# One of the four sums of K made by an accumulating DMA, in an attention kernel on one core

## The chip, the core and the metric

The kernel runs on one core of a Trainium2 chip. The core has five engines that run side by side, each with a queue of its own that it works through in order: TensorE (PE; its weight loads are listed as PEld), VectorE (DVE), ScalarE (ACT), GpSimd (POOL) and SyncE (SP). Transfers run on 16 DMA engines that all queues share. The metric is the time of one execution on the device in microseconds (us); of the kernel before there are three runs, of which the median counts.

## The reference

Attention without a mask, for eight batches of 2048 rows and a width of 512, in float32 from end to end:

```python
scores = np.matmul(q, k.transpose(0, 2, 1)) / np.sqrt(d_k)
attn_weights = special.softmax(scores, axis=-1).astype(np.float32)
return np.matmul(attn_weights, v)
```

## The kernel before

The kernel works in float16 with float32 sums in PSUM, and computes both products by a Strassen-Winograd scheme: a 2 x 2 block product is made of seven products instead of eight, from sums of the blocks. For the scores, the blocks of K are `a11, a12, a21, a22` (first index: which of two neighbouring blocks of 128 keys; second: the lower or upper half of the 512 columns) and those of Q are `b11` to `b22`. From K four sums are needed: `a21 + a22`, `a11 - a21`, `(a21 + a22) - a11`, and `a12` less the third.

K is held in four chunks of 512 keys. A chunk is loaded in float32 by POOL's queue and cast to float16 on the way (`load`, L133) into one of two staging buffers (`stage`), then transposed by a DMA of SP's queue into `kraw`, one buffer a chunk (`dma_transpose`, L159). The staging buffer comes free for a later load when that transpose has landed; Q goes the same way through the same two buffers. V is loaded by POOL's queue too (L220), without staging. In the first batch some of the transposes are done by PE.

The four sums of a chunk are made by DVE in `k_sums` (L190 to L199), one `tensor_tensor` each. L194 writes `a21 + a22` to a buffer of its own, `s1`. L195 then overwrites `a21` in place by `a11 - a21`. L196 makes `s2 = s1 - a11` and L197 `s4 = a12 - s2`. The seven products of a pair of key blocks are in `Group.product`: number 5 takes `s1` as weights, 6 `s2`, 3 `s4`, and 7 the overwritten `a21`; 1, 2 and 4 take the untouched blocks. A group's results are emptied from PSUM by ACT and DVE (L353 to L367; L364 after product 7, L367 after product 3) before the exponentials (L278).

The program is written out in one order, and each engine gets its instructions in that order; nothing reorders them later. The main loop runs over 32 quarters (`g`), four a batch, of 28 slots (and six more in which only what is left over is placed). In each slot stand, one after the other: one or two products of the scores of what comes next, the sums that a table names for the slot, products of the softmax weights with V, and then what `PLAN` names: loads and transposes for the next batch. The order of the score products over seven slots is `QORDER`: product 1 of a new group, 7 of the one before, 5 and 6 of the new one, 4 of the old one, 3 and 2 of the new one.

The tables are `SUMS` (one text for each quarter of a batch) and `SUMS_AT` (the same for the quarters 0, 1 and the last two). A word such as `k03@14` means: sum 3 in the list that `k_sums(0)` returns, at slot 14. So `k?1` to `k?4` are the four lines of that list, L194 to L197 in the kernel before. Chunks 0 and 1 of the next batch are first used in the third quarter, from slots 0 and 14 on, chunks 2 and 3 in the fourth, likewise. Words with N, L and S are sums of the softmax weights (L395 to L398), x, y, z those of an inner scheme (L588 to L591), q and v those of Q and V.

`PLAN` places, as (quarter, slot) in a batch: the loads of K at (0,18), (0,24), (1,8) and (1,16), their transposes at (1,0), (1,8), (1,20) and (2,7); the loads of Q for the next half at (2,0) and (2,15), their transposes at (2,14) and (2,26); loads of V at (0,14), (1,12), (2,6) and (2,20). POOL has besides these the additions of two output halves (L555). Where two loads stand back to back in POOL's queue, the second is issued as soon as its own waits and POOL allow.

Of the kernel before, what the change touches and what calls it, by code (L numbers as in the profile page):

```python
# [12 lines left out]
def kernel(  # L13
# [21 lines left out]
    nc = tc.nc  # L35
# [7 lines left out]
    ADD = mybir.AluOpType.add  # L43
# [9 lines left out]
    CH = 4  # L53
# [29 lines left out]
    def bank(name):  # L83
        name = "pz" if name == "py" else name
        t = psum[name].tile([P, 512], F32, tag=name)
        return t
# [10 lines left out]
    kops = []  # L97
# [78 lines left out]
    def pe_transpose(what, c, n0=0, n1=CH):  # L176
        for n in range(n0, n1, 2):
            transposed(what, c, n, 2, nc.scalar.copy if n and n0 != n else nc.vector.tensor_copy)

    def k_blocks(c):  # L180
        w = kops[c][0][:].rearrange("p (j s) c r -> p j s c r", s=2)
        return w[:, :, 0, 0:2], w[:, :, 0, 2:4], w[:, :, 1, 0:2], w[:, :, 1, 2:4]

    def q_blocks(sp):
        w = qraw[sp % 2]
        return w[:, 0:NT, 0:2], w[:, NT:2 * NT, 0:2], w[:, 0:NT, 2:4], w[:, NT:2 * NT, 2:4]

    add, sub = nc.vector.tensor_add, nc.vector.tensor_sub

    def k_sums(c):  # L190
        a11, a12, a21, a22 = k_blocks(c)
        _, s1, s2, s4 = kops[c]
        return [
            lambda: add(s1[:], a21, a22),  # L194
            lambda: sub(a21, a11, a21),  # L195
            lambda: sub(s2[:], s1[:], a11),  # L196
            lambda: sub(s4[:], a12, s2[:]),  # L197
        ]

    def t3_of(sp):  # L200

        if sp:
            return q_blocks(sp)[1]
        t = pts[1][0][1][:].rearrange("p j q -> p (j q)")[:, 0:NT * 2 * P]
        return t.rearrange("p (n c r) -> p n c r", n=NT, c=2)

    def q_sums(sp):
        b11, b12, b21, b22 = q_blocks(sp)
        t1, t2, t4 = qsum
        return [  # L210
            lambda: sub(t1[:], b12, b11),
            lambda: sub(t2[:], b22, t1[:]),
            lambda: sub(t3_of(sp), b22, b12),
            lambda: sub(t4[:], b21, t2[:]),
        ]
# [56 lines left out]
    def new_p(sp):  # L272
        left = ppool.tile([P, 2, NJ, QH], F16, tag="left", name="left")
        right = ppool.tile([P, NJ, 2, QH], F16, tag="right", name="right")
        pts[sp] = ((left[:, 0], left[:, 1]), right, left)
# [4 lines left out]
    def plain_tile(kb, half, name):  # L280

        st = bank(name)
        c, n = divmod(kb, CH)
        for dc in range(ND):
            nc.tensor.matmul(  # L285
                st[:], kops[c][0][:, n, dc, :], qraw[0][:, half * NT:(half + 1) * NT, dc, :],
                start=(dc == 0), stop=(dc == ND - 1),
            )
        left, right = pts[0][0:2]
        exp(right[:, kb // 2, kb % 2, :] if half else left[kb % 2][:, kb // 2, :], st[:])  # L290
# [19 lines left out]
    class Group:  # L310
# [6 lines left out]
        def product(self, n):  # L317
            c, j = divmod(self.j, 2)
            a11, a12, a21, a22 = k_blocks(c)
            b11, b12, b21, b22 = q_blocks(self.sp)  # L320
            _, s1, s2, s4 = kops[c]
            t1, t2, t4 = qsum
            t3 = t3_of(self.sp)
            if n == 1:
                if self.sp not in pts:
                    new_p(self.sp)
                self.left, self.right = pts[self.sp][0:2]
                self.x = bank("qx")
            elif n == 5:
                self.z = bank(self.own + "z")  # L330
            lhs, rhs, dst = {
                1: (a11, b11, "x"),
                2: (a12, b21, "y"),
                3: (s4, b22, "z"),
                4: (a22, t4, "x"),
                5: (s1, t1, "z"),
                6: (s2, t2, "x"),
                7: (a21, t3, "x"),
            }[n]
            dst = getattr(self, dst)  # L340
            for dc in range(2):
                nc.tensor.matmul(  # L342
                    dst[:], lhs[:, j, dc, :], rhs[:, :, dc, :],
                    start=(n in (1, 5) and dc == 0), stop=(dc == 1),
                    skip_group_check=True,
                )
            getattr(self, f"after{n}", lambda: None)()
# [259 lines left out]
    def fine(g, s, part):  # L607
# [38 lines left out]
        if part == 1:  # L646
            product(1, xb[:, 0:P])
            product(5, xb[:, P:P + W5])
            nc.scalar.copy(out=xa[:, 0:P + W], in_=xb[:, 0:P + W])
        elif part == 2:  # L650
            product(6, xb[:, 0:P])
            nc.scalar.copy(out=cs[:, 0], in_=xb[:, 0:P])  # L652
            product(2, xa[:, 0:P])
        elif part == 3:
            product(3, xa[:, P:P + W])
            product(7, xb[:, 0:P])
            nc.scalar.copy(out=cs[:, 1], in_=xb[:, 0:P])
            nc.vector.tensor_add(xa[:, P:H], xa[:, P:H], cs[:, 0])
            done(pa)
        else:  # L660
            product(4, xb[:, 0:P])
            nc.vector.tensor_add(xb[:, P:H], xb[:, P:H], cs[:, 1])
            done(pb)
# [17 lines left out]
    def placed(text):  # L681

        at = {}
        for word in text.split():
# [27 lines left out]
    SUMS = (  # L712
# [9 lines left out]
    )  # L722
    SUMS_AT = {
# [3 lines left out]
        ),  # L727
        1: (
            "z1@0 Z1@1 z2@1 Z2@1 Z3@2 S2@3 z4@5 Z4@5 x1@7 S3@9 z3@9 S4@9 x2@11 x3@13 x4@13 k01@15 "
            "k03@15 y1@16 y3@17 k04@18 y2@18 Y1@18 y4@18 k02@18 Y2@20 N1@21 Y4@21 Y3@22 N3@24 q1@27 "  # L730
            "q2@27"
        ),
        NP - 2: (
# [30 lines left out]
    background = deque()  # L764
# [13 lines left out]
    def sum_of(g, x):  # L778

        b, qt = divmod(g, NQT)  # L780
        sp = g // 2 + 1 + g % 2
        nb = b + (qt == NQT - 1)
        n = int(x[-1]) - 1
        if x[0] == "q":
            f = sp < NP // 2 and q_sums(sp)
        elif x[0] == "k":
            f = (b + 1 < B or g == 0) and k_sums(int(x[1]))
        elif x[0] == "v":
            f = nb < B and v_sums(nb, *map(int, x[1:-1]))
        elif x[0] in "XYZW":  # L790
            f = nb < B and vi_sums(nb, "XYZW".index(x[0]))
        elif x[0] in "xyzw":
            f = a_sums(g, "xyzw".index(x[0]))
        elif x[0] == "N":
            f = g + 1 < NP and p_sums(g + 1, "ab", 0, NE if g % 2 else NJ)
        elif x[0] == "L":
            f = p_sums(g, "ab", NE)
        elif x[0] == "S":
            f = p_sums(g, "ab")
        else:  # L800
            f = p_sums(g, x[0].lower(), NG if x[0] == "a" else 0)
        if f:
            f[n]()
# [79 lines left out]
    def step(n=1):  # L883
        for _ in range(min(n, len(background))):
            background.popleft()()


    for n, (kb, half) in enumerate([(kb, 0) for kb in range(4, 8)] + [(kb, 1) for kb in range(8)]):
        if (kb, half) == (5, 0):
            pe_transpose("k", 1, 2, 4)  # L890
        if (kb, half) == (6, 0):
            pe_transpose("q", 1)
            background.extend(q_sums(0))
        if (kb, half) == (3, 1):
            pe_transpose("k", 2)
        if (kb, half) == (6, 1):
            pe_transpose("k", 3)
            background.extend(k_sums(3))
        plain_tile(kb, half, "qz" if n % 3 == 2 else "qx")
        if (kb, half) in ((3, 1), (7, 1)):  # L900
            background.extend(k_sums(kb // CH))
        step(2)
    prev = None
    tiles = [(kb, half) for kb in range(8, 12) for half in range(2)]
# [84 lines left out]
```

## Time and profile before

| | before |
|---|---|
| time, median of 3 runs | 794.21 us (793.92 to 794.26) |
| span of the profiled execution, first to last instruction | 792.4 us |
| PE busy | 786.1 us |
| DVE busy | 712.4 us |
| ACT busy | 646.3 us |
| POOL busy | 124.1 us |
| packets of POOL's DMA queue (q0), share of 16 engines | 42.2% |
| packets of SP's DMA queue (q1), share of 16 engines | 39.0% |

The page and the views shown below come from one execution that the hardware profiler recorded. It gives a span, not a time of the kind that the three runs have; the median lies 1.8 us above it. An instruction's row has its start, its duration, engine, line and operation, what it writes and reads, and in brackets how long its engine stood idle before it, and what ended that. A row of a group has a count, the busy time and the mean, then the idle time. A row of the waits has the time waited in total, how often, and the longest. A row of a DMA queue has its packets, its megabytes and the time its packets took as a share of the 16 engines. A row of DMA issues ends with the time from issue to landing.

### The profile page before, as it was taken

The numbers are of one execution on the slowest core, as the hardware profiler recorded it, in microseconds if no ns is written. First come the engines' busy times: TensorE is split into PE (matmuls) and PEld (weight loads), VectorE is DVE, ScalarE is ACT, GpSimd is POOL, SyncE is SP. The second block draws the span as 40 slices with busy tenths as digits, with TensorE's granted clock in tenths as the row PEclk, the third lists the DMA queues.
The fourth block names the chain that finished last, engine by engine and source line by source line (L and its number), as shares of the span: only waits on it lengthen the run. The fifth ranks groups of instructions, "written<-read, shape, count | busy, mean of one in ns | idle before, by whom it ended". The sixth has DMA issues, their size and how long they took to land.

```text
span 792.4 us, 17987 instructions
## 1 busy us (share of the span) xinstructions
PE 786.1 (99%) x6574; PEld 536.6 (68%) x6574; DVE 712.4 (90%) x1562; ACT 646.3 (82%) x1339; POOL 124.1 (16%) x166
## 2 busy tenths in 40 slices
PE   9999999999999999999999999999999999999998
PEld 5556666666666666666666676666666666666686
DVE  3789999989999899998999989999899998999864
ACT  4678888888888888888988888888888888888862
POOL 4011111121121120211202121022210222100000
PEclk9999999999999999999999999999999999999999
DMA  9989991999929996399965999379991999911112
GB/s 222 180 149 187 159 192 35 175 199 166 180 43 186 209 176 134 71 195 180 172 130 106 193 189 180 82 136 200 163 202 55 151 195 178 195 35 47 49 66 95
DMA packets 206456, 116.05 MB, mean 146 GB/s; under 512 B 124320, under 2 KB 205344, under 8 KB 206368
## 3 DMA queue, kind: packets, MB, share of 16 engines
q0 software_dynamic: 49648, 49.29, 42.2%
q1 hardware_dynamic: 156432, 65.30, 39.0%
q8 instruction: 51, 0.84, 0.4%
q10 hardware_dynamic: 288, 0.33, 0.1%
q14 instruction: 37, 0.30, 0.1%
HBM read 100.73 MB, written 33.55 MB: 169 GB/s over the span
## 4 chain that ended last, share of the span: by engine, by line
PE 96%; DVE 2%; ACT 1%; issue 1%; DVEq 0%; ACTq 0%
PE t L342 45%; PE t L447 29%; PE t L634 17%; PE t L285 2%; DVE cz L367 1%; DVE ks L196 1%; PE tr L169 1%; PE tr L146 0%; PE t L853 0%; PE t L301 0%; DVE right L397 0%; ACT right L278 0%; ACT o L456 0%; ACT left L278 0%; DVE s L396 0%
## 5 line engine op out<-in xcount | busy, mean ns | idle before, releaser
L456 ACT ACTIVATE o<-t,r 128x256 f32<-128x256 f32 x314 | 143.9, 480 | 88.0 <-DVE r L482 33.2
L342 PE MATMUL t<-qraw,kraw 128*128 128x512 f16 x728 | 198.0, 379 | 0.1
L278 ACT ACTIVATE left<-t 128x512 f16<-128x512 f32 (+1 forms) x260 | 154.4, 601 | 12.0 <-PE t L342 5.8
L342 PE MATMUL t<-qs,ks 128*128 128x512 f16 x488 | 138.7, 379 | 0.1
L278 ACT ACTIVATE right<-cz 128x1024 f16<-128x1024 f32 x122 | 129.9, 1065 | 1.0 <-DVE cz L364 0.8
L342 PEld LDWEIGHTS <-kraw 128*128 128x128 f16 x976 | 87.1, 97 | 57.9 <-issue 0.6
L447 PEld LDWEIGHTS <-right 128*128 128x128 f16 x1024 | 99.5, 98 | 38.3 <-DVE right L397 2.7
L447 PEld LDWEIGHTS <-s 128*128 128x128 f16 x1072 | 102.1, 97 | 30.5 <-issue 0.3
L634 PEld LDWEIGHTS <-si 128*128 128x128 f16 x1044 | 75.4, 97 | 39.4 <-issue 1.4
L555 POOL TENSOR_TENSOR o<-o 128x256 f32<-128x256 f32 x58 | 51.1, 882 | 307.9 <-ACT o L456 221.2
L367 DVE TENSOR_TENSOR cz<-t,cz 128x512 f32<-128x512 f32 x122 | 83.8, 686 | 15.3 <-ACT o L456 6.7
L342 PEld LDWEIGHTS <-ks 128*128 128x128 f16 x732 | 67.9, 97 | 40.2 <-issue 0.2
L358 ACT COPY cz<-t 128x512 f32<-128x512 f32 x120 | 70.5, 587 | 26.2 <-PE t L342 25.2
L364 DVE TENSOR_TENSOR cz<-t,cz 128x512 f32<-128x512 f32 x122 | 83.5, 684 | 4.0 <-PE t L342 3.6
L634 PEld LDWEIGHTS <-left 128*128 128x128 f16 x928 | 66.2, 97 | 20.6
L459 DVE SCALAR_TENSOR_TENSOR o<-t,r,o 128x256 f32<-128x256 f32 x134 | 62.5, 478 | 19.0 <-ACT ci L652 6.4
L353 ACT COPY t<-t 128x512 f32<-128x512 f32 x120 | 69.9, 583 | 3.2 <-PE t L342 0.8
L447 PE MATMUL t<-vt,s 128*128 128x256 f16 (+1 forms) x560 | 72.5, 273 | 0.0
L342 PE MATMUL t<-qs,kraw 128*128 128x512 f16 x244 | 72.5, 378 | 0.0
L342 PE MATMUL t<-qraw,ks 128*128 128x512 f16 x244 | 72.4, 378 | 0.0
L361 ACT COPY cz<-t 128x512 f32<-128x512 f32 x122 | 71.2, 583 | 0.3
L634 PE MATMUL t<-vh,left 128*128 128x128 f16 x696 | 67.3, 219 | 0.0
(101 smaller groups left out, 1239.1 us busy)
## 6 DMA issues: line engine op xcount, KB each, us to landing
out_dram<-o SPq DMA_DIRECT2D x256, 128.0 KB, 2.5
vh<-in_v_dram POOLq DMA_DIRECT2D x32, 512.0 KB, 10.6
stage<-in_q_dram POOLq DMA_DIRECT2D x28, 512.0 KB, 7.1
stage<-in_k_dram POOLq DMA_DIRECT2D x28, 512.0 KB, 7.6
right<-in_q_dram POOLq DMA_DIRECT2D x2, 512.0 KB, 9.9
right<-in_k_dram POOLq DMA_DIRECT2D x2, 512.0 KB, 12.0
first<-in_q_dram SPq DMA_DIRECT2D x2, 256.0 KB, 3.7
cz<-in_q_dram SPq DMA_DIRECT2D x2, 256.0 KB, 4.7
```

The source lines that it names most:

```text
L278: nc.scalar.activation(out=out_, in_=in_, func=EXP, scale=inv_sqrt_d)
L342: nc.tensor.matmul(dst[:], lhs[:, j, dc, :], rhs[:, :, dc, :], start=(n in (1, 5) and dc == 0), stop=(dc == 1), skip_group_check=True,)
L353: f(out=self.y[:], in_=self.x[:])
L358: f(out=self.cz[:, 1, :], in_=self.z[:])
L361: nc.scalar.copy(out=self.cz[:, 0, :], in_=self.x[:])
L364: nc.vector.tensor_add(self.cz[:, 1, :], self.x[:], self.cz[:, 1, :])
L367: nc.vector.tensor_add(self.cz[:, 0, :], self.z[:], self.cz[:, 0, :])
L447: nc.tensor.matmul(dst[:, 0:width], lhs(j), rhs(j), start=(first and j == 0), stop=(j == NJ - 1), skip_group_check=True,)
L456: nc.scalar.activation(out=out_, in_=src, func=COPY, scale=r[:])
L459: nc.vector.scalar_tensor_tensor(out=out_, in0=src, scalar=r[:], in1=out_, op0=MULT, op1=ADD)
L555: nc.gpsimd.tensor_add(self.o11, self.o11, more)
L634: nc.tensor.matmul(dst, lhs[:, j, :], rhs[:, j, :], start=(n == 1 and j == 0), stop=(j == NI - 1), skip_group_check=True,)
```

## The change

`a21 + a22` is made in place, in `a21`, by a DMA of POOL's queue that reads `a22` and adds it to what is there. `a11 - a21`, which needs the old `a21`, is therefore made first and goes to the buffer that `s1` had, now called `s3`. `s2` is made from the new `a21`. For three chunks of the first batch (0, 1 and 3) the addition stays on DVE, in place; chunk 2 of that batch and all four of each later one are made by the DMA, 29 in all. Products 5 and 7 take their weights from the exchanged places. In the tables the words are placed anew: `k?2`, which was the last of a chunk's four, stands right behind `k?1`.

```diff
+    def by_dma(out_, in_):
+        nc.gpsimd.dma_start(out=out_, in_=in_, accum_op=ADD)
+
+    def k_sums(c, first=False):
         a11, a12, a21, a22 = k_blocks(c)
-        _, s1, s2, s4 = kops[c]
+        _, s3, s2, s4 = kops[c]
         return [
-            lambda: add(s1[:], a21, a22),
-            lambda: sub(a21, a11, a21),
-            lambda: sub(s2[:], s1[:], a11),
+            lambda: sub(s3[:], a11, a21),
+            lambda: add(a21, a21, a22) if first else by_dma(a21, a22),
+            lambda: sub(s2[:], a21, a11),
             lambda: sub(s4[:], a12, s2[:]),
         ]
...
-                5: (s1, t1, "z"),
+                5: (a21, t1, "z"),
                 6: (s2, t2, "x"),
-                7: (a21, t3, "x"),
+                7: (s3, t3, "x"),
...
-            background.extend(k_sums(3))
+            background.extend(k_sums(3, True))
...
-            background.extend(k_sums(kb // CH))
+            background.extend(k_sums(kb // CH, True))
```

The words of K in the tables, by quarter of a batch:

| place | before | after |
|---|---|---|
| first quarter of all (`g` 0) | k21@17 k22@18 k23@22 k24@27 | the same |
| second quarter of all (`g` 1) | k01@15 k03@15 k04@18 k02@18 | k01@15 k02@15 k03@20 k04@20 |
| second quarter | k01@11 k03@14 k04@18 k02@18 | k01@11 k02@11 k03@18 k04@18 |
| third quarter, chunk 1 | k11@14 k13@15 k14@17 k12@18 | k11@4 k12@4 k13@14 k14@15 |
| third quarter, chunk 2 | k21@17 k22@19 k23@26 k24@27 | k21@17 k22@17 k23@26 k24@27 |
| fourth quarter, chunk 3 | k31@1 k33@8 k34@10 k32@18 | k31@1 k32@1 k33@8 k34@10 |

More of the change, by code (lines that the diff above doesn't have):

```diff
@@ L188 @@
     add, sub = nc.vector.tensor_add, nc.vector.tensor_sub
-    def k_sums(c):
+    def by_dma(out_, in_):
+        nc.gpsimd.dma_start(out=out_, in_=in_, accum_op=ADD)
+    def k_sums(c, first=False):
         a11, a12, a21, a22 = k_blocks(c)
-        _, s1, s2, s4 = kops[c]
+        _, s3, s2, s4 = kops[c]
         return [
-            lambda: add(s1[:], a21, a22),
-            lambda: sub(a21, a11, a21),
-            lambda: sub(s2[:], s1[:], a11),
+            lambda: sub(s3[:], a11, a21),
+            lambda: add(a21, a21, a22) if first else by_dma(a21, a22),
+            lambda: sub(s2[:], a21, a11),
             lambda: sub(s4[:], a12, s2[:]),
@@ L320, in product @@
             b11, b12, b21, b22 = q_blocks(self.sp)
-            _, s1, s2, s4 = kops[c]
+            _, s3, s2, s4 = kops[c]
             t1, t2, t4 = qsum
@@ L729 @@
             "z1@0 Z1@1 z2@1 Z2@1 Z3@2 S2@3 z4@5 Z4@5 x1@7 S3@9 z3@9 S4@9 x2@11 x3@13 x4@13 k01@15 "
-            "k03@15 y1@16 y3@17 k04@18 y2@18 Y1@18 y4@18 k02@18 Y2@20 N1@21 Y4@21 Y3@22 N3@24 q1@27 "
+            "k02@15 y1@16 y3@17 y2@18 Y1@18 y4@18 k03@20 k04@20 Y2@20 N1@21 Y4@21 Y3@22 N3@24 q1@27 "
             "q2@27"
```

12 rows, old and new, of the table SUMS are left out of this document.

## The prediction, made before the changed kernel had run

> **What bounds the kernel now.** I read the page's busy times first, then who waits for whom, then narrow stretches of the timeline of each engine around the sums of K.
>
> ```profile
> span 792.4 us, 17987 instructions
> PE 786.1 (99%) x6574; PEld 536.6 (68%) x6574; DVE 712.4 (90%) x1562; ACT 646.3 (82%) x1339; POOL 124.1 (16%) x166
> ```
>
> PE is busy for all but 6.3 us, so work taken from another engine can win at most those. DVE, at 90%, runs just behind PE: a stall on it soon becomes a stall of PE. Two rows of the waits, one of PE's weight loads and one of POOL, show where there is no slack.
>
> ```profile
> PEld L447 <- DVE right L397: 2.7, 7, 0.4
> ```
>
> ```profile
> POOL stage L133 <- DMA kraw<-stage: 149.2, 18, 13.8
> ```
>
> Seven times, once a batch, PE waits 0.4 us for L397 on DVE: there DVE sets the pace. And POOL's in-order queue stands for up to 13.8 us at a load (L133) that needs a staging buffer back from a DMA transpose of K. The change puts DMAs into that queue, and DVE will wait for them.
>
> **The change, part by part.** *Removed:* 29 of the 32 additions `a21 + a22` on DVE (three of the first batch stay there).
>
> ```profile
> L194 DVE TENSOR_TENSOR ks<-kraw 128x512 f16<-128x512 f16 x32 | 15.7, 490 | 1.1 <-ACT kraw L172 0.8 <-DMA kraw<-stage 0.2
> ```
>
> 29 x 0.49 = 14 us of DVE's 712. I count this as nothing: PE is full beside them. If they were what PE waits for, the gain would be the 2.7 us above at most, and that wait hangs on a chain without them, shown below. *Moved, at nothing:* `a11 - a21`, same size, goes to the buffer that held the sum; PE's products 5 and 7 swap operands of equal shape.
>
> *Added:* 29 accumulating DMAs of 128 KB on POOL's queue, four a batch, each of which waits for `k?1` on DVE, and after each a wait of DVE: `k?3` reads the sum. So each is late or not by three things: what POOL does before it, what its ring still holds, and where `k?3` stands. The nearest rows for the first two are a pair of loads that POOL issues back to back (timeline of POOL; then the issues of the two, with the us to landing):
>
> ```profile
> 393.59 0.74 POOL L133 DMA_DIRECT2D stage<-in_q_dram  x1 [13.43 <-DMA kraw<-stage]
> 394.32 0.75 POOL L220 DMA_DIRECT2D vh<-in_v_dram  x1
> ```
>
> ```profile
> stage<-in_q_dram POOLq DMA_DIRECT2D x1, 512.0 KB, 7.5
> vh<-in_v_dram POOLq DMA_DIRECT2D x1, 512.0 KB, 10.3
> ```
>
> The first lands at 401.1, the second, issued 0.7 later, at 404.6: 3.5 us apart. They don't share the engines, they go one after the other. An accumulating DMA issued behind a load will land after it. How long it then takes, d, no row shows. The queues' packets in three stretches of 1 us (365 to 366, 400 to 401, 393 to 394):
>
> ```profile
> q0 software_dynamic: 163, 0.15, 89.1%
> q1 hardware_dynamic: 166, 0.04, 30.9%
> ```
>
> ```profile
> q0 software_dynamic: 198, 0.20, 122.4%
> ```
>
> ```profile
> q1 hardware_dynamic: 1133, 0.29, 127.5%
> ```
>
> POOL's queue (q0) moves 198 packets, 0.20 MB, in a us alone, 163 beside transposes. `a21` is two runs of 512 B in each of 128 partitions: 256 packets. Bounds: by bytes 0.128/0.20 = 0.65 us; if every run counts twice, being read from two places, 512/163 = 3.1 us. I take 256/198 = 1.3, since time here follows packets. And q1's transposes fall from 1133 packets to 166 beside q0, so each us that q0 works longer costs a transpose under way 0.85 us: c = 0.85 d = 1.1 (0.55 to 2.7).
>
> [...]
>
> *Place A, chunk 2, third quarter of a batch.* `k22@17` comes behind the load of q at (2,15), the one that stood 13.43 us above for the transpose of chunk 3. So POOL can issue it only at 394.33 although `k21` is done long before, and it lands d after 401.1. DVE's rows (start, us), then PE's:
>
> ```profile
> 398.75 0.72 DVE L196 TENSOR_TENSOR ks<-ks,kraw 128x512 f16<-128x512 f16 x1
> 399.50 0.43 DVE L197 TENSOR_TENSOR ks<-kraw,ks 128x512 f16<-128x512 f16 x1
> 399.84 0.42 DVE L397 TENSOR_TENSOR right<-left,right 128x512 f16<-128x512 f16 x1
> ```
>
> ```profile
> 399.38 1.32 PE L447 MATMUL t<-vh,right 128*128 128x256 f16 x8
> 400.54 0.59 PE L342 MATMUL t<-qs,ks 128*128 128x512 f16 x2
> ```
>
> `k23` (L196) keeps its place, 398.75, before the load has landed. Queued behind it are `k24` and L397, for which PE's L447 waits already, the 0.4 us above. No slack: what `k23` is late, PE is late. The seven batches differ; the first and the last of them (POOL's issue, its landing, `k23`):
>
> ```profile
> 103.06 0.74 POOL L133 DMA_DIRECT2D stage<-in_q_dram  x1 [10.53 <-DMA kraw<-stage]
> ```
>
> ```profile
> stage<-in_q_dram POOLq DMA_DIRECT2D x1, 512.0 KB, 6.8
> ```
>
> ```profile
> 110.20 0.71 DVE L196 TENSOR_TENSOR ks<-ks,kraw 128x512 f16<-128x512 f16 x1
> ```
>
> ```profile
> 680.29 0.74 POOL L133 DMA_DIRECT2D stage<-in_q_dram  x1 [12.86 <-DMA kraw<-stage]
> ```
>
> ```profile
> stage<-in_q_dram POOLq DMA_DIRECT2D x1, 512.0 KB, 5.6
> ```
>
> ```profile
> 687.07 0.71 DVE L196 TENSOR_TENSOR ks<-ks,kraw 128x512 f16<-128x512 f16 x1
> ```
>
> Landing less `k23`: 103.06 + 6.8 - 110.20 = -0.34 in the first, -1.18 in the last; worked out alike, all seven are -0.34, 1.80, -0.30, 2.34, -1.05, -1.49, -1.18. To each comes d, and c, because `k12@4` is now in front of the load of v that runs beside the transpose of chunk 3 for which POOL stands. With d + c = 2.4: 2.1 + 4.2 + 2.1 + 4.7 + 1.4 + 0.9 + 1.2 = 16.6 us.
>
> *Place B, chunk 0, second quarter.* `k02@11` comes behind the load of k at (1,8); `k03@18` takes the place that `k04` had (L197). First and last of the six like batches (issue, landing, L197), with what follows on DVE and PE in the first:
>
> ```profile
> 168.50 0.78 POOL L133 DMA_DIRECT2D stage<-in_k_dram  x1 [7.77 <-DMA kraw<-stage]
> ```
>
> ```profile
> stage<-in_k_dram POOLq DMA_DIRECT2D x1, 512.0 KB, 8.1
> ```
>
> ```profile
> 173.67 0.42 DVE L197 TENSOR_TENSOR ks<-kraw,ks 128x512 f16<-128x512 f16 x1
> ```
>
> ```profile
> 175.82 0.69 DVE L367 TENSOR_TENSOR cz<-t,cz 128x512 f32<-128x512 f32 x1 [0.42 <-ACT cz L361]
> ```
>
> ```profile
> 178.09 0.59 PE L342 MATMUL t<-qs,ks 128*128 128x512 f16 x2
> ```
>
> ```profile
> 649.37 0.78 POOL L133 DMA_DIRECT2D stage<-in_k_dram  x1 [7.87 <-DMA kraw<-stage]
> ```
>
> ```profile
> stage<-in_k_dram POOLq DMA_DIRECT2D x1, 512.0 KB, 7.9
> ```
>
> ```profile
> 654.45 0.42 DVE L197 TENSOR_TENSOR ks<-kraw,ks 128x512 f16<-128x512 f16 x1
> ```
>
> The load lands 168.50 + 8.1 - 173.67 = 2.93 us after that place, 2.82 in the last; all six: 2.93, 2.68, 0.06, 2.71, 1.31, 2.82. Here is some cover. Behind `k03` stand two short sums, `k04` and a reciprocal, then L367, which empties the bank that PE's product 5 (178.09) overwrites: L367 would start 1.2 and end 1.9 us after the landing, so PE bears a landing up to 176.2, 2.5 past the place. Per batch lateness + 1.3 - 2.5: 1.7 + 1.5 + 0 + 1.5 + 0.1 + 1.6 = 6.4 us. Without the cover it would be 20.
>
> *Chunks 1 and 3, at nothing.* `k12@4` is issued behind the load of q at (2,0), `k32@1` when `k31` and an addition of POOL are done:
>
> ```profile
> 378.64 0.78 POOL L133 DMA_DIRECT2D stage<-in_q_dram  x1 [0.65 <-issue]
> ```
>
> ```profile
> stage<-in_q_dram POOLq DMA_DIRECT2D x1, 512.0 KB, 7.9
> ```
>
> ```profile
> 387.52 0.41 DVE L194 TENSOR_TENSOR ks<-kraw 128x512 f16<-128x512 f16 x1
> ```
>
> ```profile
> 406.57 0.41 DVE L196 TENSOR_TENSOR ks<-ks,kraw 128x512 f16<-128x512 f16 x1
> ```
>
> The first lands at 386.5 + 1.3, 0.3 after `k13`'s new place (387.52, where `k11` was); its product comes two slots later. The second has v's landing, 404.6 + 2 x 1.3 = 407.2, against `k33` at 406.57 plus what PE has lost at A just before. With d = 3.1 both would add some 4 us. The first batch's own order I leave out.
>
> *The sum:* 16.6 + 6.4 = 23 on the profiled span, 815.4. The median shown, 794.2, lies 1.8 above the span; so 817.2. The bounds of d give 8.5 + 3.7 = 12 us (806) and 40 + 16 = 56 us (851); with d and c at zero 4.1 + 1.1 us would still be lost (799.5).
>
> **The rivals.** *Faster:* the accumulating DMA doesn't stand behind the load's packets.
>
> ```profile
> out_dram<-o SPq DMA_DIRECT2D x256, 128.0 KB, 2.5
> ```
>
> A store of the same 128 KB lands in 2.5 us; issued at 394.33 the sum would be there at 396.8, 1.9 before `k23`, and at B too. It decides at 4.4 us from issue to landing. DVE then has 14 us less to do, and the kernel ends at 794.2 - 2.7 = 791.5 if all the waits for L397 go. Against it stands the order in which the two loads landed, and that L397's chain at A holds none of the removed additions. [...]
>
> *No change:* in time as above, and nothing won, 794.2. For it speaks how full PE is within a batch (stretch, us, then busy time of PE, PEld, DVE, ACT and POOL):
>
> ```profile
> 351.80:447.90 96.10, 95.99 (x819) 65.55 (x817) 90.24 (x201) 82.02 (x173) 16.20 (x21) 1.00 0.89 153
> ```
>
> *Much slower:* each run is read twice and the DMA takes 3.1 us, 851. For it, only that the packets of q0 go at 163 in a us beside transposes; against it, that 256 are enough for the bytes.
>
> **How the numbers follow.** The forecast, late at A and B with d near 1.3 (799 to 832), 0.62; much slower (832 to 856) 0.18; faster 0.14; no change 0.06. 0.2%, 1.6 us, is about what a measurement of this kernel can tell from no change; so faster 0.14, same 0.06, slower 0.80. The range 798 to 842 leaves out the faster cases and the top of the slow ones; the likeliest case's own is 806 to 832.
>
> **What would show it.** In the profile after, DVE should wait for a DMA into kraw at the line of `k?3`, longest in the third quarter, and PE should stand as long for L397; fewer but similar waits in the second, none over a us for chunks 1 and 3. The accumulating DMAs of chunks 0 and 2 should land 7 to 10 us after issue, those of chunk 3 earlier. If they land in 2 to 4 us, the queueing is wrong and with it the sign; if DVE waits and PE doesn't, the cover is larger than I read it; if waits at A are over 5 us, d is.

## The result, and the profile after

| | before | after |
|---|---|---|
| time, median | 794.07 us (793.69 to 794.26, 4 runs) | 834.25 us (830.25 to 839.31, 4 runs) |
| span of the profiled execution | 792.4 us | 837.5 us |
| ratio, with its 95% interval | | 1.0508 (1.0463 to 1.0554) |

The changed kernel is slower by 40 us. The prediction had said 817.2, with 798 to 842 as its range. In the experiments below a time is the median of all runs of a kernel and a ratio is that of its fast runs, which leaves out one run of four, over 1.5% above the fastest, in two of the kernels (with 841.55 and 810.61 us). In the rows of the changed kernel every line from L190 on has moved down: `k?1` to `k?4` are L197 to L200, the DMA is L191, L342 of before is L345, L364 is L367, L367 is L370, L397 is L400 and L447 is L450. The head of its page, and its rows of POOL's and SP's DMA queues and of the new DMA:

```profile
span 837.5 us, 18029 instructions
...
PE 799.0 (95%) x6574; PEld 539.5 (64%) x6574; DVE 702.3 (84%) x1533; ACT 642.9 (77%) x1339; POOL 161.5 (19%) x195
```

```profile
q0 software_dynamic: 57536, 53.09, 45.0%
q1 hardware_dynamic: 156432, 65.30, 38.1%
```

```profile
kraw<-kraw POOLq DMA_DIRECT2D x29, 128.0 KB, 6.6
```

The change does what it says: 29 instructions fewer on DVE, 29 DMAs more, and DVE's busy time falls from 712.4 to 702.3 us. PE does the same 6574 matmuls, but stands: what isn't PE's busy time grew from 6.3 us (792.4 - 786.1) to 38.5 (837.5 - 799.0), that is by 32.2. The other 12.9 us of the 45.1 by which the spans differ are PE's busy time itself, 786.1 to 799.0. Who waits for whom, in the waits of the changed kernel:

```profile
DVE ks L199 <- DMA kraw<-kraw: 55.5, 19, 6.2
...
PEld L345 <- DMA kraw<-kraw: 16.1, 6, 3.9
...
PE t L345 <- DMA kraw<-kraw: 14.4, 6, 3.6
...
PE t L345 <- DVE cz L370: 10.8, 5, 3.5
...
PEld L450 <- DVE right L400: 3.6, 7, 1.2
```

DVE stands 55.5 us at `k?3` for the new DMA, as forecast. But PE's waits aren't where the forecast had most of them. L450 for L400, the chain of place A (chunk 2, third quarter), is 3.6 us, against 2.7 before. PE waits at L345 instead, in part for the DMA itself. DVE's timeline in one batch, at places B (chunk 0), C (as I call chunk 1 from here, `k13@14` of the third quarter) and A:

```profile
388.71 0.42 DVE L199 TENSOR_TENSOR ks<-kraw 128x512 f16<-128x512 f16 x1 [5.87 <-DMA kraw<-kraw]
...
414.57 0.43 DVE L199 TENSOR_TENSOR ks<-kraw 128x512 f16<-128x512 f16 x1 [4.89 <-DMA kraw<-kraw]
...
426.12 0.71 DVE L199 TENSOR_TENSOR ks<-kraw 128x512 f16<-128x512 f16 x1
```

Added up over the batches, DVE waits 28.2 us at B, 22.3 at C, 1.1 at A, 1.5 at chunk 3 and 2.4 once in the first batch. PE's timeline in the same batch:

```profile
390.52 0.81 PE L345 MATMUL t<-qs,kraw 128*128 128x512 f16 x2 [3.18 <-DVE cz L370]
...
414.60 1.02 PE L345 MATMUL t<-qs,kraw 128*128 128x512 f16 x2 [3.61 <-DMA kraw<-kraw]
```

The first gap is the chain foreseen for B: the DVE row L370 behind `k03` empties the bank that product 5 needs. The second chain is shorter: product 5 of chunk 1 reads the sum itself. And both matmuls took longer (0.81 and 1.02 us; 0.59 in the undisturbed rows). Stretches of 1 us of the changed kernel (busy time of PE, PEld, DVE, ACT and POOL, then PE's granted clock, DMA share and GB/s):

```profile
389.00:390.00 1.00, 0.00 (x0) 0.00 (x0) 1.00 (x5) 0.09 (x1) 0.00 (x0) 1.00 1.17 89
390.00:391.00 1.00, 0.48 (x2) 0.20 (x2) 1.00 (x3) 1.00 (x3) 0.00 (x0) 0.88 0.87 103
391.00:392.00 1.00, 0.76 (x6) 0.43 (x5) 1.00 (x3) 1.00 (x4) 0.00 (x0) 0.50 0.17 45
392.00:393.00 1.00, 1.00 (x9) 0.83 (x7) 1.00 (x2) 0.68 (x2) 0.58 (x1) 0.50 0.45 148
393.00:394.00 1.00, 1.00 (x7) 0.74 (x5) 0.00 (x0) 0.97 (x1) 0.17 (x1) 0.50 1.71 130
394.00:395.00 1.00, 1.00 (x7) 0.47 (x6) 0.62 (x2) 0.33 (x2) 0.00 (x0) 0.91 0.42 88
```

After the gap of 3.18 us PE runs at half its clock for 3.4 us. The trace has four such stretches, at 308, 390, 414 and 496; one less the granted clock, summed over slices of 1 us, is 1.7 us for each of the first three and 3.4 for the last, 8.5 in all. The kernel before has none.

Last, the landings. These are POOL's timeline and then three answers on its issues (the last number is us from issue to landing): the load of q at (2,0), chunk 1's DMA behind it, and the transpose of chunk 3 that SP issued at the same time.

```profile
400.45 0.79 POOL L133 DMA_DIRECT2D stage<-in_q_dram  x1 [1.00 <-DVE o L462]
403.03 1.19 POOL L191 DMA_DIRECT2D kraw<-kraw  x1 [1.79 <-PE t L345]
```

```profile
stage<-in_q_dram POOLq DMA_DIRECT2D x1, 512.0 KB, 6.9
```

```profile
kraw<-kraw POOLq DMA_DIRECT2D x1, 128.0 KB, 11.5
kraw<-stage SPq DMA_TRANSPOSE x1, 15.1
```

The load lands at 407.3 and the DMA, issued 2.6 us after the load's issue, at 414.5: 7.2 us behind the load, not 1.3. The transpose, issued at 402.94, is under way until 418.0.

### The profile page after: what moved, and what is told of

It is laid out like the page before. It is cut to its first block, busy times and chain, and to the rows that moved or that the text cites. A ratio compares the mean times of both kernels' runs of the same rounds, so it can differ in the third digit from the quotient of the medians.

```text
span 837.5 us, 18029 instructions
## 1 busy us (share of the span) xinstructions
PE 799.0 (95%) x6574; PEld 539.5 (64%) x6574; DVE 702.3 (84%) x1533; ACT 642.9 (77%) x1339; POOL 161.5 (19%) x195
## 3 DMA queue, kind: packets, MB, share of 16 engines
q0 software_dynamic: 57536, 53.09, 45.0%
## 4 chain that ended last, share of the span: by engine, by line
PE 73%; DMA 17%; DVE 4%; ACT 3%; issue 2%; POOL 0%; DVEq 0%; POOLq 0%; ACTq 0%
PE t L345 34%; PE t L450 23%; DMA kraw<-kraw 14%; PE t L637 12%; DMA kraw<-stage 4%; PE t L288 2%; DVE ks L199 1%; ACT right L281 1%; ACT left L281 1%; ACT o L459 1%; DVE cz L370 1%; PE tr L169 1%; PE tr L146 0%; PE t L856 0%; PE t L304 0%
## 5 line engine op out<-in xcount | busy, mean ns | idle before, releaser
L345 PE MATMUL t<-qs,kraw 128*128 128x512 f16 x488 | 147.6, 384 | 25.4 <-DMA kraw<-kraw 14.4
L345 PE MATMUL t<-qraw,ks 128*128 128x512 f16 x484 | 144.3, 380 | 1.7 <-ACT cz L361 1.2
L345 PE MATMUL t<-qraw,kraw 128*128 128x512 f16 x488 | 141.4, 379 | 0.9 <-ACT left L281 0.9
L345 PEld LDWEIGHTS <-kraw 128*128 128x128 f16 x976 | 87.4, 98 | 79.6 <-DMA kraw<-kraw 16.1
L450 PEld LDWEIGHTS <-right 128*128 128x128 f16 x1024 | 99.5, 98 | 39.2 <-DVE right L400 3.6
L450 PEld LDWEIGHTS <-s 128*128 128x128 f16 x1072 | 103.6, 99 | 32.3 <-issue 1.9
L345 PEld LDWEIGHTS <-ks 128*128 128x128 f16 x732 | 67.7, 98 | 51.6 <-issue 2.6
L370 DVE TENSOR_TENSOR cz<-t,cz 128x512 f32<-128x512 f32 x122 | 83.8, 687 | 13.5 <-ACT o L459 4.7
L367 DVE TENSOR_TENSOR cz<-t,cz 128x512 f32<-128x512 f32 x122 | 83.6, 685 | 4.7 <-PE t L345 4.3
L637 PEld LDWEIGHTS <-left 128*128 128x128 f16 x928 | 67.3, 98 | 22.9 <-issue 3.0
L450 PE MATMUL t<-vt,s 128*128 128x256 f16 (+1 forms) x560 | 74.3, 277 | 0.3 <-ACT o L459 0.3
L345 PE MATMUL t<-qs,ks 128*128 128x512 f16 x244 | 73.6, 384 | 0.0
L364 ACT COPY cz<-t 128x512 f32<-128x512 f32 x122 | 71.0, 582 | 1.8 <-PE t L345 1.8
L450 PE MATMUL t<-vh,s 128*128 128x257 f16 x512 | 68.1, 276 | 0.1
```

Source lines behind the costliest of these rows:

```text
L345: nc.tensor.matmul(dst[:], lhs[:, j, dc, :], rhs[:, :, dc, :], start=(n in (1, 5) and dc == 0), stop=(dc == 1), skip_group_check=True,)
L364: nc.scalar.copy(out=self.cz[:, 0, :], in_=self.x[:])
L367: nc.vector.tensor_add(self.cz[:, 1, :], self.x[:], self.cz[:, 1, :])
L370: nc.vector.tensor_add(self.cz[:, 0, :], self.z[:], self.cz[:, 0, :])
L450: nc.tensor.matmul(dst[:, 0:width], lhs(j), rhs(j), start=(first and j == 0), stop=(j == NJ - 1), skip_group_check=True,)
L637: nc.tensor.matmul(dst, lhs[:, j, :], rhs[:, j, :], start=(n == 1 and j == 0), stop=(j == NI - 1), skip_group_check=True,)
```

## Experiments

Each run stands beside runs of the kernel before on the same chip; ratios are to those. Where only one line differs from the changed kernel, the diff is against it.

**What was there to win, and what do the tables cost?** First all sums on DVE, in place, in the changed kernel's tables:

```diff
-            lambda: add(a21, a21, a22) if first else by_dma(a21, a22),
+            lambda: add(a21, a21, a22),
```

> The changed kernel with all 32 sums a21 + a22 on DVE, in place, at the changed tables' slots: no accumulating DMA, no wait for one. If the loss is DVE's wait for the DMAs (theory W) or their traffic (theory T): 793 to 796 us, within 0.3% of the kernel before. If it is the exchange of the buffers or the new places of the sums in the tables (theory P): 805 to 834.

798.49 us (797.89 to 799.94; 1.0049, 1.0034 to 1.0064): some 4 us slower than before, a little over what was expected. Then the chunk 1 and 2 words of the third quarter near their old slots, with the same edit:

```diff
-        "q3@0 q4@4 L1@4 z1@4 k11@4 k12@4 S2@6 ... x4@13 k13@14 k14@15 N1@16 y1@16 k21@17 k22@17 ..."
+        "q3@0 q4@4 L1@4 z1@4 S2@6 ... x4@13 k11@14 k12@14 k13@15 N1@16 y1@16 k14@17 k21@17 y2@18 k22@19 ..."
```

> K's sums all on VectorE in place, as in the run with 798.49, but with chunk 1's and chunk 2's words in the third quarter's table near the slots that they had before the change. If the 4 us of that run came from the new early slots: 793 to 796. If they came from the sum being made in place (VectorE writes a21's own tile and a11 - a21 goes to the buffer): 797 to 800 again.

795.13 us (1.0013, 1.0004 to 1.0022). So 3.4 of those 4 us are the new slots of the third quarter with DVE's work in them, and the in-place form costs at most 1. And with the addition left out altogether:

```diff
-            lambda: add(a21, a21, a22) if first else by_dma(a21, a22),
+            lambda: add(a21, a21, a22) if first else None,
```

> The changed kernel with K's addition a21 + a22 left out altogether, on VectorE and on Pool's queue alike, for the same 29 chunks; the third of K's products' sums lacks a22 there. The new places in the tables stay. It shows what the change could bring at most, if the accumulating DMA cost nothing and landed at once. Theory that TensorE is full and VectorE's spared 29 x 0.43 = 12 us were never on the path: 791 to 797, no VectorE wait for a DMA into kraw from the second batch on. Rival, that the spared VectorE time is worth something: below 788.

794.86 us (1.0008, 0.9999 to 1.0017). The head of its page:

```profile
span 793.1 us, 17958 instructions
...
PE 786.3 (99%) x6574; PEld 536.5 (68%) x6574; DVE 703.7 (89%) x1533; ACT 644.5 (81%) x1339; POOL 124.5 (16%) x166
```

DVE has 8.7 us less to do than before (712.4), and PE stands no less: 6.8 us of 793.1, against 6.3. So a DMA that cost nothing and landed at once would have won nothing over the kernel before. The same tables with the additions on DVE took 798.49: the new slots cost 3.6 us only when DVE adds in them, which the changed kernel doesn't do after the first batch.

**What does the traffic cost by itself?** All sums on DVE, and beside them a DMA of the same kind, size and place whose result nobody reads as the sum:

```diff
+        def both():
+            add(a21, a21, a22)
+            if not first:
+                by_dma(s3[:], a22)
...
-            lambda: add(a21, a21, a22) if first else by_dma(a21, a22),
+            both,
```

> As the run with all sums on DVE, but at the same 29 places an accumulating DMA of the same size follows on POOL's queue, which adds a22 into s3; only product 7 reads that, 13 us or more later, so nothing on DVE waits for it (product 7 then computes with a11 - a21 + a22). W: 793 to 797, since nobody waits. T (the DMAs delay loads and transposes, and these the engines): 805 to 835.

805.23 us (803.21 to 806.76; 1.0134, 1.0093 to 1.0176), 6.7 above the run without the DMAs: above what theory W had said and at the lower end of T's range. So the traffic has a price of its own, though a small one beside 40 us. DVE doesn't wait for them at `k?3`, but PE waits once, an effect of this kernel's extra writes to `s3` (waits; L350 is the line of the products):

```profile
PE t L350 <- DMA ks<-kraw: 1.6, 1, 1.6
```

That is 1.6 of the 6.7. Along with the rest, transposes land later: those of chunk 3 took 13.0 to 15.1 us, against 9.4 to 11.5 without the DMAs.

**One place at a time.** Chunk 2 alone (A), the largest term of the prediction:

```diff
-            lambda: add(a21, a21, a22) if first else by_dma(a21, a22),
+            lambda: by_dma(a21, a22) if c == 2 and not first else add(a21, a21, a22),
```

> The changed kernel with the accumulating DMA for chunk 2 alone (place A, 8 DMAs); chunks 0, 1 and 3 are summed by VectorE in place, as in the run with 798.49. It puts the prediction's largest term on its own. Theory that A was hidden in the changed kernel by the stall at chunk 1 just before it: without that stall VectorE waits at k23 in most batches, 10 to 18 us in all, and the time is 809 to 817 (798.5 plus 16.6 by the prediction's term is 815). Rival, that chunk 2's sum comes in time in these tables whatever stands before: under 2 us of waits, and at most 801.

807.11 us (804.32 to 811.93; 1.0171, 1.0127 to 1.0215), 8.6 above the run with all on DVE. DVE's wait at `k23` is back in four of seven batches (0.94, 0.69, 3.58 and 0.50 us, 5.7 in all), in the very chain that the prediction named. DVE's timeline of this kernel at the longest, then PE's, then PE's stretches of 1 us:

```profile
407.79 0.42 DVE L199 TENSOR_TENSOR ks<-kraw 128x512 f16<-128x512 f16 x1 [3.58 <-DMA kraw<-kraw]
408.24 0.42 DVE L200 TENSOR_TENSOR ks<-kraw,ks 128x512 f16<-128x512 f16 x1
408.59 0.42 DVE L400 TENSOR_TENSOR right<-left,right 128x512 f16<-128x512 f16 x1
```

```profile
409.06 0.61 PE L450 MATMUL t<-vh,right 128*128 128x256 f16 x2 [3.48 <-DVE right L400]
```

```profile
409.00:410.00 1.00, 0.94 (x4) 0.54 (x5) 1.00 (x4) 0.75 (x2) 0.19 (x1) 0.50 1.19 235
410.00:411.00 1.00, 1.00 (x6) 0.54 (x5) 0.96 (x3) 0.65 (x2) 0.53 (x1) 0.50 1.27 182
```

No slack, as said: DVE 3.58 late, PE 3.48 late, and the half clock on top. But the waits stay below the 10 to 18 us that were expected, and the time came out at about half of the term (8.6 of 16.6, from runs that spread over 7.6 us). In all seven batches the DMA lands 0.7 to 0.9 us after the load of q. Chunk 0 alone (B), the same edit with `c == 0`:

> The changed kernel with the accumulating DMA for chunk 0 alone (place B, 7 DMAs); the others by VectorE in place. The prediction's term for B was 6.4 us, by which the time is 803 to 807. By what the changed kernel's trace shows (VectorE waits at k03 of 28 us, gaps of PE of 12 to 13 us, and the half clock after the longest of them) it is 809 to 818, with waits at k03 of 20 to 30 us.

815.54 us (813.42 to 820.12; 1.0278, 1.0245 to 1.0311), 17.1 above the run with all on DVE. Waits, and PE's timeline in one batch:

```profile
DVE ks L199 <- DMA kraw<-kraw: 26.1, 7, 4.8
```

```profile
183.22 0.59 PE L345 MATMUL t<-qs,kraw 128*128 128x512 f16 x2 [2.09 <-DVE cz L370]
184.27 0.59 PE L637 MATMUL t<-ti,si 128*128 128x128 f16 x4 [0.46 <-ACT t L652]
```

That is in the range expected. DVE's wait at `k03` is 4.78 here, PE's gap 2.09: a cover of 2.7 us, near the 2.5 foreseen. But in each of the six batches a second gap of 0.46 follows, ended by ACT's L652, which the kernel before doesn't have; why ACT is late there was not followed up. Here the half clock follows too (PE's clock is 0.50 from 184 to 187).

**Do the places cover one another?** B's wait taken away by moving `k03` and `k04` to the end of the second quarter:

```diff
-k03@18 k04@18
+k03@24 k04@25
```

> The changed kernel with k03 and k04 of the usual second quarter moved from slot 18 to slots 24 and 25, 5 us later; they are first used 3 slots into the next quarter. W: the waits of DVE in the second quarter (about 27 of the 55.5 us, PE idle of some 12 us and the half clock after the long ones) go, and 812 to 824 us remain, the third quarter's waits as they were or a little longer. T or P: 830 to 840, unchanged.

841.55 us (832.53 to 847.71; 1.0547, 1.0474 to 1.062): a miss. No wait of DVE at the moved `k03` is left (only the one of `g` 1, whose words stayed), and the time is not shorter. The waits of this kernel:

```profile
DVE ks L199 <- DMA kraw<-kraw: 46.9, 18, 7.6
...
PE t L345 <- DMA kraw<-kraw: 24.5, 7, 6.3
```

C's waits grew from 22.3 to 33.4 us, and PE's from 14.4 to 24.5. From the issue of C's DMA to DVE's arrival at `k13` it is 6.7 us in every batch of both kernels, so DVE is no earlier at it. What grew is the DMA's time to landing, from 9.8 to 11.4 us on average: the load of q ahead of it now lands 5.1 us after that issue on average, where it was 3.6. What B had lost in time had gone to that load. Next, C taken away: `k11` and `k12` before the load of q, in the second quarter, and `k13` where it was:

```diff
 second quarter (and that of g 1)
+k11@22 k12@22        (g 1: @23)
 third quarter
-k11@4 k12@4
```

> The changed kernel with k11 and k12 moved from slot 4 of the third quarter to slot 22 of the second (slot 23 in the first batch), so that the DMA of chunk 1 is queued ahead of the load of q at (2,0) and has some 18 slots until k13. W: the waits for chunk 1 (22 us of DVE's 55.5, some 16 us of PE idle and the half clock after the long ones) go; but their delay had covered the DMA of chunk 2, where 1 to 3 us a batch come back: 812 to 828 us. T or P: 830 to 840.

821.43 us (821.07 to 828.19; 1.0352, 1.03 to 1.0404), as expected. C's waits are gone, B's stay (27.5 us), and 4.3 us at A are back. With both edits:

> Both moves together: k03, k04 at slots 24 and 25 and k11, k12 at slot 22 of the second quarter. W (each wait of DVE for a DMA costs, and one place covers the next): with chunks 0 and 1 out of the way only chunk 2's place is left, where 1 to 3 us a batch come back as predicted: 805 to 817 us. If the loss isn't tied to these places: 825 to 840.

820.64 us (817.91 to 825.75; 1.0332, 1.028 to 1.0383), above what was expected. Its waits:

```profile
DVE ks L199 <- DMA kraw<-kraw: 23.8, 11, 6.3
...
PE t L450 <- DVE right L400: 16.4, 7, 6.2
```

Now nearly all of it is A: DVE waits 17.1 us at `k23`, and PE stands 16.4 for L400. Then A moved as well, `k21` and `k22` to slot 5, before the load of q at (2,15):

```diff
 third quarter, on top of the last two edits
-k21@17 k22@17
+k21@5 k22@5
```

> As the run before, and k21, k22 moved from slot 17 to slot 5 of the third quarter, so that the DMA of chunk 2 is queued ahead of the load of v at (2,6) and doesn't stand behind the load of q at (2,15). W: no wait of DVE for a DMA over 1 us in any batch but the first; 794 to 801 us, the traffic's cost alone. Rival (the queue is too full for four more DMAs a batch, whatever their place): 808 to 820.

810.61 us (803.73 to 816.3; 1.0175, 1.0105 to 1.0245). The runs fall into two pairs: 803.7 and 806.1 lie between the two ranges, 815.2 and 816.3 in the rival's, so neither is settled. The profile is that of 816.3. In it DVE's waits of 17.7 us stand mostly at chunk 3, four of 2.2 to 4.8: there `k32` is issued while the load of v and a transpose still run, and lands 7 us later. In that execution the place that is freed hands the stall to the next.

**Is it that the DMA adds?** The same DMA as a plain copy of `a22` over `a21`:

```diff
-        nc.gpsimd.dma_start(out=out_, in_=in_, accum_op=ADD)
+        nc.gpsimd.dma_start(out=out_, in_=in_)
```

> The changed kernel with plain copies a21 <- a22 in place of the accumulating ones, same size, queue and places (so the third sum lacks a21). If being an accumulation is what makes the DMA of chunk 1 land 4 to 8 us after the load ahead of it: that falls to about 1 us, and 805 to 820 us. If any DMA of that shape would wait so beside the transposes: 828 to 840.

845.19 us (842.18 to 852.78; 1.0654, 1.0598 to 1.0709): above both ranges. These are POOL's rows at C in the batch shown above, with the answer on the copy's issue, and then the same of the batch before that one:

```profile
403.60 0.79 POOL L133 DMA_DIRECT2D stage<-in_q_dram  x1 [2.94 <-DVE si L591]
404.44 0.71 POOL L191 DMA_DIRECT2D kraw<-kraw  x1
```

```profile
kraw<-kraw POOLq DMA_DIRECT2D x1, 128.0 KB, 7.9
```

```profile
298.51 0.78 POOL L133 DMA_DIRECT2D stage<-in_q_dram  x1
302.33 0.71 POOL L191 DMA_DIRECT2D kraw<-kraw  x1 [3.05 <-PE t L345]
```

```profile
kraw<-kraw POOLq DMA_DIRECT2D x1, 128.0 KB, 9.1
```

In the first, the copy is issued 0.84 us behind the load and lands at 412.3, 1.4 us behind it (410.9). In the second it is issued 3.8 us behind the load, lands at 311.4, and the load at 305.7: 5.7 us. The second is the usual case: in six of the seven batches the copy is issued 2.2 to 3.9 us behind the load and lands 4.5 to 5.9 us after it, where the adding DMA lands 4.1 to 8.3 after it. So a plain copy is late at C as well, as the second theory had it. Adding makes a part of it, 1.5 us on average (6.2 against 4.7). Whether the rest comes from the later issue or from the transposes that run beside it, these runs don't separate.

C's waits fall from 22.3 to 14.4 us. But A's are back in all seven batches (1.7 to 3.6 us each, 17.0 in all), and the total wait of DVE is 63.2 us. C's stall is shorter, and chunk 3's transposes, for which POOL stands ahead of A, took 13.1 to 16.0 us here, against 10.3 to 15.1 in the changed kernel. So a somewhat sooner landing at C doesn't pay.

**Chunk 3 alone**, in the tables of before (7 DMAs, `k32` moved to slot 1 behind `k31`, the other chunks as before):

```diff
+        if c == 3 and not first:
+            return [
+                lambda: sub(s1[:], a11, a21),
+                lambda: by_dma(a21, a22),
...
-        "z1@0 k31@1 S2@2 ... y3@17 k32@18 y2@18 ..."
+        "z1@0 k31@1 k32@1 S2@2 ... y3@17 y2@18 ..."
```

> The kernel before, with the change for chunk 3 alone (7 accumulating DMAs, buffers exchanged for that chunk, k31 and k32 at slot 1, tables otherwise as before). Chunk 3's DMA is issued alone, 3.6 to 4.7 us from issue to landing, and k33 comes 5 us later. W: 793 to 797 us, a wait of some 0.5 us in single batches. If a DMA on POOL's queue costs wherever it is put: 800 and more.

795.24 us (1.0009, 1.0000 to 1.0018). The load of v ahead of this DMA has landed at its issue in four batches of seven and is near its end in two more; the DMA lands 4.2 us after its issue (median), 6.3 in the one batch in which the load still had 3.9 us to go. DVE waits for it in four batches, 3.7 us in all, and PE stands 0.55 behind DVE in one. It wins nothing. No version beat the kernel before.

## Why the prediction was right, and where its steps were off

The sign, the bound and the mechanism held. DVE's time was not on the path: left out at no cost, the additions win nothing (of the 14 us that the prediction took off DVE's busy time, 8.7 were measured). The DMA goes through POOL's in-order queue and lands after the load ahead of it (all 29 of them, by 0.2 us or more); DVE stands at `k?3` (55.5 us) and PE behind DVE (10.8 us for L370). The time lies within the range but 2 us above the likeliest case's own (806 to 832), where the forecast had put a DMA of 3.1 us; that is not what the runs showed. That the sum came near is in good part luck: the place that was to lose 16.6 of the 23 us lost next to nothing, while chunk 1, put at nothing, lost some 13 (below). The terms, one by one:

- **A, 16.6 us.** In the changed kernel it is 1.1. The step that failed is the one that took each place as if the others didn't exist. C's stall lies between POOL's wait for chunk 3's transpose and `k23`: before, 17.7 us lay between the issue of that transpose (381.06) and `k23` (398.75); after, 23.2 (402.94 to 426.12). In that time the DMA lands. In the run with both B and C moved it is 17.4 to 17.8 in all seven batches, and A has 17.1 us of waits. Alone, A is 5.7 us of DVE's waits and 8.6 of the time.
- **d, 1.3 us.** Behind the load at A it measured 0.7 to 1.0, near the lower bound. The packets were counted rightly: q0 has 272 more for each DMA ((57536 - 49648)/29, from the queue's row after and the same row before), not 512. c was 1.1; chunk 3's transposes took 12.2 us on average, 10.5 before, so 1.7. With 0.8 in place of d + c = 2.4 (chunk 1 has no DMA in the run with A alone), the prediction's own seven differences give 0.5, 2.6, 0.5, 3.1, 0, 0, 0, that is 6.7 us. A alone measured 0.9, 0.7, 0, 3.6, 0, 0, 0.5, or 5.7: near in the sum, less so batch by batch. The 1.3 took time to follow packets, and the landings don't bear that out: 272 packets in 0.7 to 1.0 us are more than the 198 a us from which it was worked out. Adding is dearer than copying at A, by the same measure: the plain copy landed there 0.3 to 0.4 us after the load.
- **B, 6.4 us.** Alone, it cost 17.1. The first gaps of PE were sized about right: 2.09, 1.16, 0.66, 1.88, none and 1.88, 7.7 us in six batches. Left out were a gap of 1.20 in the first batch, a second gap of 0.46 in every batch, and the half clock, 1.7. Together these make some 13 of the 17; the rest stays open.
- **Chunk 1 at nothing.** The step that failed is "386.5 + 1.3". The DMA there isn't issued directly behind the load but 2.6 to 3.9 us after it, since it waits for `k11` (in each batch its issue follows the end of `k11` by 0.6 us, though the row's bracket names PE), and it runs beside chunk 3's transpose: it landed 4.1 to 8.3 us after the load. Which of the two makes it late stays open; a plain copy is late there too. DVE waits 22.3 us for it, PE's matmuls 14.4. What this place costs alone was not run; from the run without it (821.43) to the changed kernel (834.25) it is 13 us, with A's cover counted against it.
- **Chunk 3 at nothing** held in the changed kernel (1.5 us of DVE's waits) and alone. It failed, in the execution profiled, once the other three were moved.
- **Two terms were missing:** the traffic without any wait of DVE's, up to 6.7 us, and the half clock after stalls, 8.5 us in the changed kernel's trace.

Of the signs that the prediction named, "longest in the third quarter, and PE should stand as long for L397" was wrong, "none over a us for chunks 1 and 3" was wrong for chunk 1, and "waits at A over 5 us" did not occur in the changed kernel. From the second batch on chunk 0's DMAs landed 7.6 to 10.8 us after their issue, about as foreseen; chunk 2's took 3.9 to 7.2, less than the 7 to 10 foreseen; chunk 3's were earlier, as said.

How 834 comes about, as far as the runs show: without the additions the changed tables take 794.9, so the 39 us above that come with the DMAs. Up to 7 go with their traffic alone, and the rest with DVE's waits, the half clock among it. A and B alone make 8.6 + 17.1 = 25.7; with all 29 DMAs in the queue and C's moved out of the way it is 22.9 (821.43 - 798.49). How traffic and waits share the rest can't be read from these runs, since the waits move with the landings.

## What to carry to other kernels

Before moving work off an engine, leave it out and time that: here the answer was 794.9 against 794.3, so no DMA in these tables could have won anything. The DMA moved to POOL's in-order queue took its landing here from what stood ahead of it (0.7 to 1.0 us behind the load at A, 4.1 to 8.3 at C, where the part of the transposes beside it stayed open), and its reader took that wait into its own queue (55.5 us of DVE's); look for every reader, also those with a microsecond or two of room (B, with a cover of 2.5 us foreseen, cost 17.1). Don't add up stalls that follow one another: here the first gave the second its time (1.1 us of waits at A behind 22.3 at C), and moving the first away brought the second back (17.1 at A with B and C moved). And where a trace is to show a cause, look at every batch: at C the one batch with an early copy was the exception.

## What the runs showed of the hardware that was not expected

**Half clock after a stall.** In the changed kernel, matmuls after gaps of 3.18, 3.40, 3.46 and 3.61 us ran at a granted clock of 0.50 for 3.4 to 6.8 us, after one of 3.24 they did not, and after 2.49 or less they did not either; with B alone, gaps of 2.09 and 0.46 close together went with it. So it isn't a fixed length of gap. The four stretches begin at 308.84, 390.76, 414.66 and 496.58 (the clock read in steps of 0.02 us), that is 24, 7 and 24 times 3.413 us apart, and each lasts one or two times 3.41: in this trace they lie on one grid. With windows of 3.413 us laid on it, the four drops to half follow windows in which PE was idle for 2.31, 3.17, 3.35 and 2.71 us, and no full-speed window that another one at full speed followed had more than 1.82 (the first 15 and the last 8 us of the trace are left out). The gap of 3.24 lies across two windows, which had 1.50 and 1.75 us of idle time. The last stretch goes on for a second window, though PE was idle for only 0.78 us of its first. Each stretch loses 1.7 us or a multiple (with A alone and with B alone one of 1.7 each, in the changed kernel three of 1.7 and one of 3.4). So here the stalls of 3.40 and 3.61 us cost PE over 5 us each.

**A small DMA behind a load.** In the changed kernel the 128 KB that are added landed, at A, 0.7 to 1.0 us after the load that they followed (at B 0.2 to 0.8, once 5.1, beside chunk 1's transpose), and as a plain copy 0.3 to 0.4. For chunk 3, with the loads ahead landed, they took 3.6 to 4.7 us from issue, though a transpose was under way each time. At C, issued later behind a load and beside transposes, the adding DMA landed 4.1 to 8.3 us after the load and the copy 4.5 to 5.9, once 1.4. The same 128 KB are 272 packets of POOL's queue when they are added and 48 when they are copied (51040 packets on the copy's page, 49648 before). Adding also holds POOL longer at the issue, 1.19 us in the row above against 0.71 for the copy.
